# Conditioning by columns, rotary tables loaded early, the context's keys after the first gate tile, and squares added up on TensorE

## The chip, the cores and the metric

The kernel runs on one core of a Trainium2 chip. The metric is the device time of one execution in microseconds (us), as the median of several executions; lower is better. The engines are named as the profile names them: PE (TensorE's matmuls), PEld (its weight loads), DVE (VectorE), ACT (ScalarE), POOL (GpSimd), SP (the engine that issues the DMAs).

## What is computed

Two layers of a diffusion backbone over 1024 latent tokens of width 1024, with 256 context tokens. The change touches only the start of the first layer: the modulation from the two conditioning vectors `c` and `c_ctx`, the RMSNorms of latents and context, and keys and values. Cut to that, the reference is:

```
def rms_norm(x, g):
    y = x * lax.rsqrt(jnp.mean(x * x, axis=-1, keepdims=True) + EPS)
    return y * g

def adaln(cvec, w_mod, b_mod):
    return jnp.split(jax.nn.silu(cvec) @ w_mod + b_mod, 6, axis=-1)

# layer 0
sh1, sc1, gt1, sh2, sc2, gt2 = adaln(c, w_mod[0], b_mod[0])
csh1, csc1, ...              = adaln(c_ctx, w_mod[0], b_mod[0])
xm = rms_norm(h, g_mix[0]) * (1.0 + sc1) + sh1        # 1024 latent tokens
xc = rms_norm(ctx, g_mix[0]) * (1.0 + csc1) + csh1    # 256 context tokens
q, k, v, su, sv = split_in_proj(xm @ w_in)
q  = apply_axial_rope(rms_norm(q, q_gain), rope)
k  = apply_axial_rope(rms_norm(k, k_gain), rope)
kc, vc = jnp.split(xc @ w_in[:, k and v columns], 2)
kc = rms_norm(kc, k_gain)                             # no rotation
attn = block_attention(q, concat([kc, k]), concat([vc, v]))
sg   = spatial_gating(gelu(su), gelu(sv), w_sp, b_sp)
h = h + gt1 * (concat([attn, sg]) @ w_out)            # then the FFN, then layer 1
```

## The kernel before

Features lie on the 128 partitions (eight tiles, k = 0 to 7) and tokens run along the free axis; the latents come in two halves of 512 tokens, `xA` and `xB`, the context as `xhC` (eight tiles of 256). Every product of wide matrices is split in high and low parts and made of three matmuls (`mm3`, L180).

**Conditioning** (L245 to L314). The first 2048 of the modulation's columns (shift and scale) are needed first. Their weights `wma` come in eight blocks of 1 MB, one for each k. For three quarters of the columns, PE multiplies with `s2v[:, k, :]` (the two silu'd vectors, two columns) as the stationary operand and 512 columns of weights as the moving one, into three rows `mps` (L277); for the last quarter DVE forms weighted sums `macc` (L254, L256), whose columns PE adds up with a vector of ones (`col_sums`, L185). ACT copies the rows `mps` out (`mrow`, L305), PE turns them in twelve transposes (L308), and `mcol` then holds all shifts and scales as columns. DVE makes `mod`, `modc` and the gains `gp` of it (L299, L310, L311).

**Norms.** `sumsq` squares each tile on ACT (L207) and adds the squares on DVE (L211); `rstd_bcast` has PE add up the columns (`ps_v`, L185), DVE scales (`nv`, L196), POOL takes the power (`nr`, L140), and PE spreads the result over the partitions (`rb`, L200). That is done for `xA` inside the conditioning loop, later for the context and for `xB` (`normalize`, L219 to L227, which also writes the modulated high and low parts `xcm` and `xm[1]`). `xA` gets its modulation by `shift` and `parts` (L386 to L397) and becomes `xm[0]`.

**Tables.** `gains` and `rope` are loaded after that (L371, L375), and POOL multiplies them to four tables (`tab`, L380), which the keys (`rotate`, L442, L445) need.

**Keys, values, gate** (L514 to L526). `wkv` is the weight of keys and values; `kv_tile(kt)` handles 128 tokens (24 matmuls of 256 columns); kt 0 and 1 are the context, 2 to 5 the first half, 6 to 9 the second. `su_half(0, wu, 0)` is the first gate tile `u` (48 matmuls of 512 columns, `ups`). The order written is kt 2 to 5, kt 0 and 1, `u`, kt 6 to 9.

Two things set the order of the work: each engine runs its own list in order, and a scheduler of the tile framework makes these lists from the program, by its own estimates, before anything runs. Pools limit how far ahead an engine may go: squares and the later modulation weights `wmb` share three buffers (`npool`), weights `w` share four (`wpool`) with the `wma` blocks k = 4 to 7, and unconverted weights `raw` have three.

Of the kernel before, what the change touches and what calls it, by code (L numbers as in the profile page):

```python
# [18 lines left out]
P = 128  # L19
# [33 lines left out]
def hybrid_kernel(  # L53
# [35 lines left out]
    def htile(name="h", n=HALF):  # L89
        return hpool.tile([P, NB], F32, name=name, tag="h")[:, 0:n]  # L90
# [4 lines left out]
    def xtile(n=HALF, name="x"):  # L95
        return xpool.tile([P, NB], F32, name=name, tag="x")[:, 0:n]
# [86 lines left out]
    def col_sums(out, a):  # L183

        nc.tensor.matmul(out=out, lhsT=a, rhs=ones[:, 0:1], start=True, stop=True)  # L185


    def rstd_bcast(s, n, scale):

        at = [min(o, n - P) for o in range(0, n, P)]  # L190
        nj = len(at)
        ps = psc(nj, "ps_v")
        for j, o in enumerate(at):
            col_sums(ps[:, j:j + 1], s[:, o:o + P])
        v = sm(nj, "nv")
        nc.vector.tensor_scalar(out=v, in0=ps, scalar1=scale, scalar2=EPS, op0=ALU.mult, op1=ALU.add)  # L196
        r = rsqrt_small(v, nj, "nr")
        rb = psc(n, "rb")
        for j, o in enumerate(at):
            nc.tensor.matmul(out=rb[:, o:o + P], lhsT=r[:, j:j + 1].broadcast_to([P, P]), rhs=ident, start=True, stop=True)  # L200
        return rb

    def sumsq(tiles, n, alloc=ntile):
        s = None
        for t in tiles:
            q = alloc(n, "sq")
# [9 lines left out]
    def new_xm(half):  # L216
        xm[half] = [blk("xm") for _ in range(KD)]

    def normalize(tiles, n, g, b, outs, inplace):  # L219

        rb = rstd_bcast(sumsq(tiles, n), n, 1.0 / D)
        for k, t in enumerate(tiles):
            y = t if inplace else ntile(n, "xh")
            (hi, lo), gk, bk = outs(k), g[:, k:k + 1], b[:, k:k + 1]
            nc.vector.scalar_tensor_tensor(out=y, in0=t, scalar=gk, in1=rb, op0=ALU.mult, op1=ALU.mult)
            nc.scalar.activation(hi, y, AF.Identity, bias=bk)  # L226
            nc.vector.scalar_tensor_tensor(out=lo, in0=y, scalar=bk, in1=hi.bitcast(F32), op0=ALU.add, op1=ALU.subtract)  # L227

    def normalize_xm(half, tiles, g, b, cs=slice(0, HALF), inplace=False):
        normalize(tiles, cs.stop - cs.start, gp[:, g:g + KD], mod[:, b:b + KD],  # L230
                  lambda k: (xm[half][k][:, 0, cs], xm[half][k][:, 1, cs]), inplace)

    def load_pairs(half, k0, n):
        out = []
        for k in range(k0, k0 + n):
            if k % 2 == 0:
                t = blk("xp", F32)
            nc.sync.dma_start(out=t[:, k % 2, :], in_=xT[half, k])
            out.append(t[:, k % 2, :])
        return out  # L240
# [5 lines left out]
    s2 = const.tile([P, 16], F32, name="s2")  # L246
    nc.scalar.activation(s2, col(C_C2, 16), AF.Silu)
    s2v = s2.rearrange("p (k two) -> p k two", two=2)
    mps = [psa(name="mps") for _ in range(3)]
    macc = [xtile(name="macc") for _ in range(2)]  # L250

    def weighted_add(acc, w, cs, first):
        if first:
# [2 lines left out]
            nc.vector.scalar_tensor_tensor(out=acc, in0=w, scalar=cs, in1=acc, op0=ALU.mult, op1=ALU.add)  # L256

    xA = []
    for k in range(KD):
        if k < 4:  # L260
            ws = []
            for i in range(2):
                t = blk("wma", F32)
                nc.sync.dma_start(out=t, in_=wm_a[k][:, i * 1024:(i + 1) * 1024].rearrange("p (a b) -> p a b", a=2))
                ws += [t[:, 0, :], t[:, 1, :]]
        else:
            t = wpool.tile([P, 2048], F32, name="wma", tag="w")
            nc.sync.dma_start(out=t, in_=wm_a[k])
            ws = [t[:, j * 512:(j + 1) * 512] for j in range(4)]
        if k in (1, 3):  # L270
            xA += load_pairs(0, 2 * (k - 1), 4)
        if k == 5:
            wqueue.append(w_in[2])
            wqueue.extend(w_in[{"q": 0, "u": 3, "v": 5}[kind] + g] for kind, g in STAGES)
            wqueue.extend(w_out[g] for _ in range(2) for g in range(4))
        for j in range(3):
            nc.tensor.matmul(out=mps[j][0:2, :], lhsT=s2v[:, k, :], rhs=ws[j], start=(k == 0), stop=(k == KD - 1))  # L277
        for e in range(2):
            weighted_add(macc[e], ws[3], s2v[:, k, e:e + 1], k == 0)
        if k == 4:  # L280
            rbA = rstd_bcast(sumsq(xA, HALF), HALF, 1.0 / D)
    mcol = psc(32, "mcol")
    for i in range(4):
        for e in range(2):
            col_sums(mcol[:, 24 + 2 * i + e:25 + 2 * i + e], macc[e][:, i * P:(i + 1) * P])
    wready.append(prep(wqueue.popleft()))
    for t in xA:
        nc.vector.tensor_tensor(out=t, in0=t, in1=rbA, op=ALU.mult)
# [10 lines left out]
        nc.vector.scalar_tensor_tensor(out=gp[:, dst:dst + 8], in0=sc, scalar=1.0, in1=col(g, 8),  # L299
                                       op0=ALU.add, op1=ALU.mult)  # L300

    mrow = []
    for j in range(3):
        t = htile("mrow")
        nc.scalar.activation(t[0:2, :], mps[j][0:2, :], AF.Copy)  # L305
        mrow.append(t)
    for i in range(12):
        nc.tensor.transpose(mcol[:, 2 * i:2 * i + 2], mrow[i // 4][0:2, (i % 4) * P:(i % 4 + 1) * P], ident[0:2, 0:2])  # L308
    mcv = mcol.rearrange("p (i two) -> p i two", two=2)
    nc.vector.tensor_tensor(out=mod[:, 0:16], in0=mcv[:, :, 0], in1=col(C_BMOD, 16), op=ALU.add)  # L310
    nc.vector.tensor_tensor(out=modc, in0=mcv[:, :, 1], in1=col(C_BMOD, 16), op=ALU.add)  # L311
# [58 lines left out]
    gt = htile("gt")  # L370
    nc.sync.dma_start(out=gt[:, 0:256], in_=gains.partition_broadcast(P))  # L371
    rt = []
    for i in range(2):
        t = htile("rt")
        nc.sync.dma_start(out=t, in_=rope[i])  # L375
        rt.append(t)

    def table(i, g):
        t = htile("tab")
        nc.gpsimd.tensor_tensor(out=t.rearrange("p (t d) -> p t d", d=HD),  # L380
                                in0=rt[i].rearrange("p (t d) -> p t d", d=HD),
                                in1=gt[:, g * HD:(g + 1) * HD].unsqueeze(1).broadcast_to([P, 8, HD]), op=ALU.mult)
        return t
# [15 lines left out]
    for k in range(0, KD, 2):  # L399
# [1 line left out]
        shift(k + 1)  # L401
        parts(k + 1)
        parts(k)
    kC, kS, qC, qS = table(0, 2), table(1, 3), table(0, 0), table(1, 1)
    xcm = [blk("xcm") for _ in range(4)]

    def xc_dst(k):
# [1 line left out]
        sl = slice((k % 2) * CTX, (k % 2 + 1) * CTX)  # L409
        return b[:, 0, sl], b[:, 1, sl]  # L410

    normalize(xhC, CTX, gp[:, 8:16], modc[:, 0:8], xc_dst, True)
    new_xm(1)
    normalize_xm(1, xB, 0, SH1, inplace=True)

    def lat(k, tt):
        b = xm[tt // 4][k]
# [783 lines left out]
```

## Time and profile before

| | us |
|---|---|
| median of three runs | 2373.87 (2371.97 to 2375.66) |
| the profiled execution | 2372.76 |
| its span on the core | 2371.0 |

| engine | busy us | share of the span |
|---|---|---|
| PE | 2327.0 | 98% |
| PEld | 1978.2 | 83% |
| DVE | 1628.5 | 69% |
| ACT | 918.5 | 39% |
| POOL | 411.1 | 17% |

The profile gives, for each stretch, how long an engine was busy and which clock TensorE was granted: 1.00 is 2.4 GHz, 0.50 is 1.2 GHz. A float32 matmul stands in it as two records. A timeline row is a run of like instructions: start, length, engine, line, what is written and read, shapes, count, and in brackets how long the engine had idled before and what ended that. The two RMSNorms, the modulation and the keys lie in the first 90 of 2371 us.

### The profile page before, as it was taken

What the parts mean: (1) busy time and instruction counts of PE and PEld (TensorE: products, weight loads), DVE (VectorE), ACT (ScalarE), POOL (GpSimd) and SP (SyncE); (2) the same over time, 40 slices, a digit from 0 to 9 for tenths busy, and PEclk for the clock granted to TensorE, in tenths of its full rate; (3) what the DMA queues carried; (4) which work ended last, traced back from release to release, by engine and by line L of the source; (5) the groups of instructions that cost most, each with busy time, mean ns of one, the idle gap of its engine ahead of it and who ended that gap; (6) DMA issues with size and microseconds to landing.
All of it is one profiled execution on the core that took longest, in us unless ns stands there. A gap on an engine that the chain in (4) does not pass through costs nothing.

```text
span 2371.0 us, 31670 instructions
## 1 busy us (share of the span) xinstructions
PE 2327.0 (98%) x12396; PEld 1978.2 (83%) x12396; DVE 1628.5 (69%) x2515; ACT 918.5 (39%) x1480; POOL 411.1 (17%) x405
## 2 busy tenths in 40 slices
PE   7999899999999999999999999999999999999998
PEld 3899677777888888888888788888878989999998
DVE  6887777656545666447999966999986555444357
ACT  4542688843211222234333455333445433222222
POOL 2362677820000000001112300002230000000000
PEclk9899999999999999999999999999999999999999
DMA  8451000042222455332222242222233222222222
GB/s 307 136 194 55 19 1 1 6 148 96 101 77 89 160 194 174 121 126 88 94 93 89 91 166 98 89 98 90 97 98 121 96 96 89 90 90 89 90 90 98
DMA packets 79573, 245.68 MB, mean 104 GB/s; under 512 B 8512, under 2 KB 12864, under 8 KB 78912
## 3 DMA queue, kind: packets, MB, share of 16 engines
q1 hardware_dynamic: 79424, 243.66, 30.4%
q8 instruction: 97, 1.59, 0.3%
q14 instruction: 52, 0.43, 0.1%
HBM read 235.24 MB, written 8.39 MB: 103 GB/s over the span
## 4 chain that ended last, share of the span: by engine, by line
PE 73%; DVE 12%; issue 2%; POOL 1%; ACT 1%; DMA 0%; DVEq 0%; ACTq 0%; POOLq 0%
PE gu L180 35%; PE fo L180 17%; PE pw L180 8%; DVE conv L999 7%; PE wo L180 4%; DVE w L113 2%; PE mx L628 2%; PE st L650 1%; PE st L649 1%; PE o L676 1%; PE o L674 1%; PE o L675 1%; POOL pacc L993 1%; DVE h L791 0%; DVE conv L1002 0%
## 5 line engine op out<-in xcount | busy, mean ns | idle before, releaser
L180 PE MATMUL gu<-xm,w 128*128 128x512 f32 (+2 forms) x5280 | 997.8, 350 | 1.9 <-ACT xm L226 1.9
L180 PEld LDWEIGHTS gu<-xm,w 128*128 128x128 f32 x5280 | 854.4, 188 | 135.0 <-ACT xm L226 2.1
L112 ACT ACTIVATE w<-raw 128x1024 fp32r<-128x1024 f32 x324 | 340.6, 1056 | 556.7 <-issue 237.7
L113 DVE TENSOR_TENSOR w<-raw,w 128x1024 fp32r<-128x1024 f32 x324 | 406.8, 1259 | 192.4 <-ACT w L112 191.8
L180 PE MATMUL fo<-act,w 128*128 128x512 f32 (+2 forms) x2640 | 499.8, 350 | 1.5 <-DVE act L113 1.5
L180 PEld LDWEIGHTS fo<-act,w 128*128 128x128 f32 x2640 | 428.3, 189 | 65.7 <-DVE act L113 1.9
L999 DVE SCALAR_TENSOR_TENSOR conv<-glu,pc,conv 128x496 f32<-128x496 f32 (+1 forms) x400 | 316.6, 836 | 0.3
L791 DVE SCALAR_TENSOR_TENSOR h<-fo,mod,h 128x264 f32<-128x264 f32 (+2 forms) x256 | 159.6, 631 | 96.7 <-PE fo L180 95.9
L993 POOL TENSOR_TENSOR pacc<-pacc,ptmp 128x496 f32<-128x496 f32 (+1 forms) x64 | 109.0, 1703 | 450.7 <-ACT pacc L989 398.3
L180 PE MATMUL pw<-xm,w 128*128 128x512 f32 x768 | 178.7, 394 | 0.0
L180 PEld LDWEIGHTS pw<-xm,w 128*128 128x128 f32 x768 | 144.1, 188 | 33.5
L841 DVE TENSOR_TENSOR silu<-gu,silu 128x512 f32<-128x512 f32 (+2 forms) x110 | 63.8, 580 | 141.0 <-PE gu L180 140.8
L840 ACT ACTIVATE silu<-gu 128x512 f32<-128x512 f32 (+2 forms) x110 | 56.2, 511 | 260.4 <-PE gu L180 260.4
L140 POOL TENSOR_TENSOR nr<-nv,mhalf 128x4 f32<-128x4 f32 (+2 forms) x16 | 16.4, 1027 | 803.3 <-DVE nv L196 803.3
L630 DVE TENSOR_REDUCE mp<-mx 128x1 f32<-128x512 f32 (+1 forms) x192 | 112.1, 598 | 24.6 <-PE mx L628 21.6
L112 ACT ACTIVATE act<-silu 128x512 fp32r<-128x512 f32 (+2 forms) x110 | 59.1, 537 | 143.6 <-DVE silu L841 143.6
L665 POOL TENSOR_TENSOR pb<-p,pb 128x512 fp32r<-128x512 f32 x80 | 104.3, 1304 | 5.3
L256 DVE SCALAR_TENSOR_TENSOR acc<-raw,s,acc 128x512 f32<-128x512 f32 x84 | 62.9, 749 | 45.2 <-DMA raw<-in_wm_b_dram 44.1
L180 PE MATMUL pw<-sw,w 128*128 128x264 f32 (+1 forms) x576 | 91.4, 320 | 0.0
L180 PE MATMUL wo<-cat,w 128*128 128x512 f32 x384 | 89.9, 394 | 0.7 <-DVE cat L113 0.7
L969 POOL MEMSET glu<- 128x15 f32 x16 | 0.9, 112 | 510.6 <-PE fo L180 510.6
L180 PEld LDWEIGHTS pw<-sw,w 128*128 128x128 f32 x576 | 83.0, 188 | 7.2
(169 smaller groups left out, 2450.3 us busy)
## 6 DMA issues: line engine op xcount, KB each, us to landing
raw<-in_ffn_in_dram SPq DMA_DIRECT2D x164, 512.0 KB, 3.6
raw<-in_ffn_out_dram SPq DMA_DIRECT2D x82, 512.0 KB, 3.6
raw<-in_wm_b_dram SPq DMA_DIRECT2D x48, 512.0 KB, 3.7
raw<-in_pw_dram SPq DMA_DIRECT2D x48, 512.0 KB, 3.7
wmb<-in_wm_b_dram SPq DMA_DIRECT2D x64, 256.0 KB, 2.8
raw<-in_w_out_dram SPq DMA_DIRECT2D x16, 512.0 KB, 3.6
raw<-in_w_in_dram SPq DMA_DIRECT2D x14, 512.0 KB, 4.6
wma<-in_wm_a_dram SPq DMA_DIRECT2D x8, 512.0 KB, 7.9
```

The source lines that it names most:

```text
L112: nc.scalar.activation(dst_hi, src, AF.Copy)
L113: nc.vector.tensor_tensor(out=dst_lo, in0=src, in1=dst_hi.bitcast(F32), op=ALU.subtract)
L180: nc.tensor.matmul(out=ps, lhsT=a, rhs=b, start=(i == 0), stop=(i == n - 1))
L256: nc.vector.scalar_tensor_tensor(out=acc, in0=w, scalar=cs, in1=acc, op0=ALU.mult, op1=ALU.add)
L628: pin(nc.tensor.matmul(out=ps, lhsT=b[:, 0, j * P:(j + 1) * P], rhs=kst1[:, kv, o:o + n], start=True, stop=True))
L630: chained(nc.vector.tensor_reduce(out=mp[:, 3 * j + s:3 * j + s + 1], in_=ps, axis=AX.X, op=ALU.max))
L665: chained(eng.tensor_tensor(out=t[:, 1, :], in0=p, in1=t[:, 0, :].bitcast(F32), op=ALU.subtract))
L791: nc.vector.scalar_tensor_tensor(out=h, in0=ps, scalar=gc, in1=h, op0=ALU.mult, op1=ALU.add)
L840: nc.scalar.activation(sg, ps, AF.Silu)
L841: nc.vector.tensor_tensor(out=sg, in0=ps, in1=sg, op=ALU.mult)
L993: nc.gpsimd.tensor_tensor(out=pacc, in0=pacc, in1=tmp, op=ALU.add)
L999: nc.vector.scalar_tensor_tensor(out=out, in0=g[:, t:t + n], scalar=wc(t), in1=out, op0=ALU.mult, op1=ALU.add)
```

## The change

Four edits, none of which alters what is computed.

1. The rows `mps`, the sums `macc`, the copies `mrow` and the transposes go. For every k PE multiplies 16 times with a 128x128 block of the weights as the stationary operand and the two columns `s2v[:, k, :]` as the moving one, straight into `mcol`, which is accumulated over k: 128 matmuls of two columns.
2. The loads of `gains` and `rope` and the four table products move up into the loop, to k = 1.
3. `su_half(0, wu, 0)` is written ahead of the context's `kv_tile(0)` and `kv_tile(1)`.
4. The norms of the context and of `xB` no longer add squares on DVE: `square_sums` has PE multiply each tile of squares, as 128x128 stationary blocks, with one column of ones, accumulating over the eight tiles: 16 such column sums for the context and 32 for `xB`, in place of 2 and 4.

```diff
+    def square_sums(tiles, n):
+        at = [min(o, n - P) for o in range(0, n, P)]
+        ps = psc(len(at), "ps_v")
+        for i, t in enumerate(tiles):
+            q = ntile(n, "sq")
+            nc.scalar.activation(q, t, AF.Square)
+            for j, o in enumerate(at):
+                nc.tensor.matmul(out=ps[:, j:j + 1], lhsT=q[:, o:o + P], rhs=ones[:, 0:1], start=(i == 0 and j == 0),
+                                 stop=(i == len(tiles) - 1), skip_group_check=True)
+        return ps, at
...
-        rb = rstd_bcast(sumsq(tiles, n), n, 1.0 / D)
+        rb = rstd_bcast((sums or sumsq)(tiles, n), n, 1.0 / D)
...
-    mps = [psa(name="mps") for _ in range(3)]
-    macc = [xtile(name="macc") for _ in range(2)]
+    mcol = psc(32, "mcol")
...
+        if k == 1:
+            gt = htile("gt")
+            nc.sync.dma_start(out=gt[:, 0:256], in_=gains.partition_broadcast(P))
+            rt = []
+            for i in range(2):
+                t = htile("rt")
+                nc.sync.dma_start(out=t, in_=rope[i])
+                rt.append(t)
+            kC, kS, qC, qS = table(0, 2), table(1, 3), table(0, 0), table(1, 1)
...
-        for j in range(3):
-            nc.tensor.matmul(out=mps[j][0:2, :], lhsT=s2v[:, k, :], rhs=ws[j], start=(k == 0), stop=(k == KD - 1))
-        for e in range(2):
-            weighted_add(macc[e], ws[3], s2v[:, k, e:e + 1], k == 0)
+        for i in range(16):
+            nc.tensor.matmul(out=mcol[:, 2 * i:2 * i + 2], lhsT=ws[i // 4][:, (i % 4) * P:(i % 4 + 1) * P],
+                             rhs=s2v[:, k, :], start=(k == 0 and i == 0), stop=(k == KD - 1),
+                             skip_group_check=True)
...
-    mcol = psc(32, "mcol")
-    for i in range(4):
-        for e in range(2):
-            col_sums(mcol[:, 24 + 2 * i + e:25 + 2 * i + e], macc[e][:, i * P:(i + 1) * P])
...
-    mrow = []
-    for j in range(3):
-        t = htile("mrow")
-        nc.scalar.activation(t[0:2, :], mps[j][0:2, :], AF.Copy)
-        mrow.append(t)
-    for i in range(12):
-        nc.tensor.transpose(mcol[:, 2 * i:2 * i + 2], mrow[i // 4][0:2, (i % 4) * P:(i % 4 + 1) * P], ident[0:2, 0:2])
...
-    normalize(xhC, CTX, gp[:, 8:16], modc[:, 0:8], xc_dst, True)
+    normalize(xhC, CTX, gp[:, 8:16], modc[:, 0:8], xc_dst, True, square_sums)
     new_xm(1)
-    normalize_xm(1, xB, 0, SH1, inplace=True)
+    normalize_xm(1, xB, 0, SH1, inplace=True, sums=square_sums)
...
+    wu = next_w()
+    su_half(0, wu, 0)
     for kt in range(0, 2):
         kv_tile(kt)
     flush()
-    wu = next_w()
-    su_half(0, wu, 0)
```

The scheduler orders the first 110 us anew. The first place is PE during the conditioning. It stood so (a row is a run of like instructions with its count; `mps` and `mcol` are the conditioning, `ps_v` column sums of squares, `rb` a norm's spreading, `kvps` keys and values):

```order
L277 MATMUL mps<-wma,s_101 2x512 x12
L185 MATMUL ps_v<-ones,sq 128x1 x4
L277 MATMUL mps<-wma,s_101 2x512 x3
L200 MATMUL rb<-ident,nr 128x128 x4
L277 MATMUL mps<-wma,s_101 2x512 x9
L185 MATMUL mcol<-ones,macc 128x1 x8
L308 MATMUL mcol<-ident,mrow 128x2 x12
L180 MATMUL kvps<-w,xm 128x256 x30
```

and stands so now:

```order
L314 MATMUL mcol<-s_101,wma 128x2 x80
L185 MATMUL ps_v<-ones,sq 128x1 x4
L314 MATMUL mcol<-s_101,wma 128x2 x14
L218 MATMUL rb<-ident,nr 128x128 x4
L314 MATMUL mcol<-s_101,wma 128x2 x34
L196 MATMUL ps_v<-ones,sq 128x1 x10
```

The `rb` of `xA` has moved behind 14 of the 16 matmuls of k = 5, and ten of the context's column sums stand between the conditioning and the first `kvps`. The second place is PE from there to the `rb` of `xB`. Before, behind the 30 `kvps` (first the context's sums and `rb`, then its keys and values, `kvps<-w,xcm`, with the sums and the `rb` of `xB` among them):

```order
L185 MATMUL ps_v<-ones,sq 128x1 x2
L180 MATMUL kvps<-w,xm 128x256 x38
L200 MATMUL rb<-ident,nr 128x128 x2
L180 MATMUL kvps<-w,xm 128x256 x28
L180 MATMUL kvps<-w,xcm 128x256 x24
L185 MATMUL ps_v<-ones,sq 128x1 x4
L180 MATMUL kvps<-w,xcm 128x256 x19
L200 MATMUL rb<-ident,nr 128x128 x4
```

and now, behind 22 `kvps` and `ups` matmuls, the context's other six sums and two `kvps`:

```order
L180 MATMUL kvps<-w,xm 128x256 x23
L218 MATMUL rb<-ident,nr 128x128 x2
L196 MATMUL ps_v<-ones,sq 128x1 x12
L180 MATMUL kvps<-w,xm 128x256 x11
L196 MATMUL ps_v<-ones,sq 128x1 x4
L180 MATMUL kvps<-w,xm 128x256 x6
L196 MATMUL ps_v<-ones,sq 128x1 x12
L180 MATMUL kvps<-w,xm 128x256 x7
L196 MATMUL ps_v<-ones,sq 128x1 x4
L180 MATMUL kvps<-w,xm 128x256 x25
L218 MATMUL rb<-ident,nr 128x128 x4
```

The 32 sums of `xB` lie in four lots among the `kvps` of kt 2 to 5; the context's `kvps` have left this piece and follow the 48 `ups` behind it. The third place is ACT from the squares of `xA` on. Before:

```order
L207 ACTIVATE sq<-xp 128x512 x8
L112 ACTIVATE w<-raw 128x1024 x2
L305 ACTIVATE mrow<-mps 2x512
L207 ACTIVATE sq<-xc 128x256 x3
L305 ACTIVATE mrow<-mps 2x512 x2
L207 ACTIVATE sq<-xc 128x256 x3
L392 ACTIVATE xp<-xp,mod,gp 128x512
```

and now (`w` is a weight's high part, `xp<-xp,mod,gp` the first `shift` of `xA`):

```order
L225 ACTIVATE sq<-xp 128x512 x8
L194 ACTIVATE sq<-xc 128x256 x2
L112 ACTIVATE w<-raw 128x1024
L194 ACTIVATE sq<-xc 128x256
L112 ACTIVATE w<-raw 128x1024 x3
L402 ACTIVATE xp<-xp,mod,gp 128x512
L194 ACTIVATE sq<-xc 128x256
L406 ACTIVATE xm<-xp 128x512
```

All four weight conversions now stand ahead of the first `shift`; each writes into a buffer that a `wma` block (k = 4, 5, 6, 7) holds until PE has read it. On DVE the first low part `w` now stands ahead of the `nv` that the `rb` of `xA` hangs on. Behind the first 110 us PE's order is the same as before.

## Rows read from the trace of the kernel before

**Rows 1.** Windows by stage: stretch, length, busy of PE, PEld, DVE, ACT, POOL, clock, DMA.
```profile
0.00:41.00 41.00, 30.58 (x92) 8.62 (x92) 23.71 (x40) 11.95 (x20) 5.47 (x10) 0.96 0.97 371
41.00:78.00 37.00, 29.56 (x171) 28.27 (x172) 32.31 (x73) 21.23 (x50) 15.30 (x12) 0.72 0.38 133
78.00:228.00 150.00, 149.91 (x1073) 140.12 (x1071) 127.72 (x316) 58.94 (x164) 65.80 (x87) 1.00 0.41 135
228.00:258.00 30.00, 23.09 (x147) 20.07 (x146) 23.26 (x55) 13.50 (x23) 17.09 (x17) 0.89 0.17 54
258.00:2371.00 2113.00, 2093.89 (x10921) 1781.15 (x10919) 1421.53 (x2036) 812.91 (x1224) 307.45 (x280) 1.00 0.29 96
```

**Rows 2.** Timeline of PE from 5 to 50 us, the conditioning.
```profile
5.94 8.20 PE L277 MATMUL mps<-wma,s 128*2 128x512 f32 x12 [5.94 <-DMA wma<-in_wm_a_dram]
...
23.87 1.05 PE L185 MATMUL ps_v<-ones,sq 128*128 128x1 f32 x8 [3.09 <-DVE sq L211]
...
30.30 7.89 PE L277 MATMUL mps<-wma,s 128*2 128x512 f32 x18
38.12 1.95 PE L185 MATMUL mcol<-ones,macc 128*128 128x1 f32 x16
...
44.16 6.13 PE L180 MATMUL kvps<-w,xm 128*128 128x256 f32 x30 [3.26 <-ACT xm L396]
```

**Rows 3.** Timeline of PE from 63 to 136 us.
```profile
63.75 5.12 PE L180 MATMUL kvps<-w,xcm 128*128 128x256 f32 x22 [2.57 <-DVE xcm L227]
68.86 1.84 PE L185 MATMUL ps_v<-ones,sq 128*128 128x1 f32 x8
71.37 4.42 PE L180 MATMUL kvps<-w,xcm 128*128 128x256 f32 x19 [0.67 <-ACT qn L433]
75.60 1.55 PE L200 MATMUL rb<-ident,nr 128*128 128x128 f32 x8
...
82.12 6.96 PE L180 MATMUL ups<-xm,w 128*128 128x512 f32 x29
...
117.01 19.09 PE L180 MATMUL qps<-w,xm 128*128 128x256 f32 x159
```

**Rows 4.** Windows, PE alone: stretch, length, busy, granted clock, DMA.
```profile
45.00:49.00 4.00, 4.00 (x20) 0.50 0.23 93
...
64.00:68.00 4.00, 4.00 (x19) 0.50 0.04 6
69.00:71.00 2.00, 1.70 (x8) 0.50 0.40 134
72.00:76.00 4.00, 4.00 (x20) 0.50 0.46 159
78.00:82.00 4.00, 4.00 (x19) 1.00 0.55 180
```

**Rows 5.** Timeline of PEld, two of the first weight loads.
```profile
11.02 0.13 PEld L277 LDWEIGHTS mps<-wma,s 128*2 128x2 f32 x1 [0.73 <-issue]
...
12.26 0.09 PEld L277 LDWEIGHTS mps<-wma,s 128*2 128x2 f32 x1 [0.34 <-issue]
```

**Rows 6.** Timeline of ACT from 34 to 44 us.
```profile
34.24 1.06 ACT L112 ACTIVATE w<-raw 128x1024 fp32r<-128x1024 f32 x1 [0.19 <-DMA raw<-in_w_in_dram]
...
37.00 1.01 ACT L207 ACTIVATE sq<-xc 128x256 f32<-128x256 f32 x3
...
41.88 0.80 ACT L392 ACTIVATE xp<-xp,mod,gp 128x512 f32<-128x512 f32 x1
...
42.96 1.15 ACT L396 ACTIVATE xm<-xp 128x512 fp32r<-128x512 f32 x2
```

**Rows 7.** Timeline of DVE: weights' low parts, and the scaling of `xB`.
```profile
36.77 2.35 DVE L113 TENSOR_TENSOR w<-raw,w 128x1024 fp32r<-128x1024 f32 x2
...
79.33 5.35 DVE L225 SCALAR_TENSOR_TENSOR xp<-xp,gp,rb 128x512 f32<-128x512 f32 x8
```

**Rows 8.** Timeline of POOL: the first power, and the tables.
```profile
25.97 1.03 POOL L140 TENSOR_TENSOR nr<-nv,mhalf 128x4 f32<-128x4 f32 x1 [20.76 <-DVE nv L196]
44.97 10.11 POOL L380 TENSOR_TENSOR tab<-rt,gt 128x512 f32<-128x512 f32 x4 [17.96 <-DMA rt<-in_rope_dram]
```

More of the change, by code (lines that the diff above doesn't have):

```diff
@@ L185, in col_sums @@
         nc.tensor.matmul(out=out, lhsT=a, rhs=ones[:, 0:1], start=True, stop=True)
+    def square_sums(tiles, n):
[8 more added lines that the diff above has]
+        return ps, at
     def rstd_bcast(s, n, scale):
+        if isinstance(s, tuple):
+            return rstd_of(*s, n, scale)
         at = [min(o, n - P) for o in range(0, n, P)]
@@ L194, in rstd_bcast, with rstd_of @@
             col_sums(ps[:, j:j + 1], s[:, o:o + P])
+        return rstd_of(ps, at, n, scale)
+    def rstd_of(ps, at, n, scale):
+        nj = len(at)
         v = sm(nj, "nv")
@@ L217, in new_xm, with normalize @@
         xm[half] = [blk("xm") for _ in range(KD)]
-    def normalize(tiles, n, g, b, outs, inplace):
-        rb = rstd_bcast(sumsq(tiles, n), n, 1.0 / D)
+    def normalize(tiles, n, g, b, outs, inplace, sums=None):
+        rb = rstd_bcast((sums or sumsq)(tiles, n), n, 1.0 / D)
         for k, t in enumerate(tiles):
@@ L227, in normalize, with normalize_xm @@
             nc.vector.scalar_tensor_tensor(out=lo, in0=y, scalar=bk, in1=hi.bitcast(F32), op0=ALU.add, op1=ALU.subtract)
-    def normalize_xm(half, tiles, g, b, cs=slice(0, HALF), inplace=False):
+    def normalize_xm(half, tiles, g, b, cs=slice(0, HALF), inplace=False, sums=None):
         normalize(tiles, cs.stop - cs.start, gp[:, g:g + KD], mod[:, b:b + KD],
-                  lambda k: (xm[half][k][:, 0, cs], xm[half][k][:, 1, cs]), inplace)
+                  lambda k: (xm[half][k][:, 0, cs], xm[half][k][:, 1, cs]), inplace, sums)
     def load_pairs(half, k0, n):
@@ L258, in hybrid_kernel, with table @@
     xA = []
+    def table(i, g):
+        t = htile("tab")
+        nc.gpsimd.tensor_tensor(out=t.rearrange("p (t d) -> p t d", d=HD),
+                                in0=rt[i].rearrange("p (t d) -> p t d", d=HD),
+                                in1=gt[:, g * HD:(g + 1) * HD].unsqueeze(1).broadcast_to([P, 8, HD]), op=ALU.mult)
+        return t
     for k in range(KD):
@@ L368, in hybrid_kernel @@
     v2 = kvpool.tile([P, NKT * 2, HD], F32R, name="v2")
[L370 to L383, printed above, removed]
     new_xm(0)
@@ L403, in hybrid_kernel @@
         parts(k)
-    kC, kS, qC, qS = table(0, 2), table(1, 3), table(0, 0), table(1, 1)
     xcm = [blk("xcm") for _ in range(4)]
```

## The prediction

> **What bounds the kernel now.** I read the windows by stage first [rows 1]. From 258 us to the end PE is busy 2093.9 of 2113 us at the full clock, and from 78 to 228 us 149.9 of 150: work that leaves DVE or ACT there is worth nothing, and what the change can win or lose has to come from the first 78 us. There PE is idle or slow: 30.6 of the first 41 us busy, then 29.6 of 37 at a mean clock of 0.72. Next, PE's own timeline of that part [rows 2, 3]. Conditioning starts at 5.94, when the first weights land, and ends 3.26 us before 44.16, so at 40.90; the first key matmul starts at 44.16. From there the 96 matmuls of kt 2 to 5, the 48 of the context and the 48 of the first gate tile `u` last until 82.12 + 6.96 = 89.1. Last, the clock [rows 4]: 0.50 from 45 to 49 and again from 64 to 76, though PE was busy in nearly all of that. So three times are to be worked out: the end of the conditioning (40.9), the first key matmul (44.2), and the end of these 192 matmuls (89.1). Behind that PE is dense, and whatever the third time moves, the end moves.
>
> **Prices.** A column sum (two records: each loads 128x128 weights, then moves one column) costs 1.95/8 = 0.244 us at the full clock [rows 2] and 1.84/4 = 0.46 at 0.50 [rows 3, 4]. The new `mcol` matmuls have the same weights and move two columns instead of one; both ends of their price are these, 0.244 and 0.46. A matmul of 256 columns costs 19.09/159 = 0.120, one of 512 columns 6.96/29 = 0.240 [rows 3]. The old form cost 7.89/9 = 0.88 for each of three matmuls per k, 2.6 us [rows 2]; the new one costs 16 x 0.244 = 3.9 or 16 x 0.46 = 7.4. So PE's share of the conditioning grows in either case, and what leaves DVE (`macc`) was not what PE waited for at the end.
>
> **Which clock?** The first weight loads follow each other at half the later pace (0.73 us of issue time before the one at 11.02, 0.34 before the one at 12.26 [rows 5]), so PE starts at 1.2 GHz and comes to 2.4 only after some 5 us of moving 512 columns at a time. In the new program there is no such stretch before the first key matmul. What do column sums do to the clock? The best row is the stretch from 63.75 [rows 3, 4]: key matmuls, then eight records of column sums from 68.86 to 70.7, an idle of 0.67 us, key matmuls again; the clock stays at 0.50 all through, until after 76, 12 us after the start, while from 71.37, where only matmuls with many columns follow, it takes about 5 us. I take it that a stretch of nothing but these narrow matmuls leaves the clock at 1.2 GHz. The Trainium skill ("TensorE: Matmul & The Clock Gate", What's actually happening) says that the clock is set by how busy PE has recently been, without telling weight loads from columns; by that, a dense stretch of narrow matmuls would raise it, and the sum would be the first rival's 2385 instead of 2409. No row here shows such a stretch as long as the new one.
>
> **The change, part by part.**
>
> *A, the end of the conditioning.* 128 x 0.46 = 58.9 us, and inside it four column sums (1.84) and one `rb` (1.55 [rows 3]): 5.94 + 62.3 = 68.2. No wait adds to that: at 371 GB/s [rows 1] all conditioning weights, with `xA` and the 0.64 MB of tables now ahead of them (11.4 MB), have landed by about 31 us, and PE comes to the last block at 60.8. 68.2 against 40.9: +27.3. The copies, transposes and `macc` sums that go (some 2.8 us behind the last `mps`) are in these two ends.
>
> *B, to the first key matmul.* PE has ten column sums of the context in front of it, 4.6 us at half clock. Beside it ACT must convert the last weight (its buffer is held until the last `mcol` matmul), 1.06, then `shift` 0.80, two squares 0.34 each, two high parts 0.57 each [rows 6]: 3.7. So 4.6 against 3.26: +1.3, first key matmul at 72.8.
>
> *C, the 192 matmuls.* Before: 89.1 - 44.2 = 44.9. Now, at full clock: 144 x 0.120 = 17.3, 48 x 0.240 = 11.5, the remaining 38 column sums x 0.244 = 9.3, six `rb` matmuls 2.3: 40.4. On top: the clock needs about 5 us to rise from 72.8, which loses 2.5. Then the piece with the 32 sums of `xB`: 7.8 us of sums with 2.9 of key matmuls strewn in, and 25 key matmuls (3.0) behind. If the clock doesn't fall it loses nothing; if the whole piece runs at half, 13.7; I take 7.5, about the middle, because the clock needs some us to fall and the last 25 matmuls to raise it. Behind the `rb` of `xB`, DVE scales `xB` (5.35 [rows 7]) and makes its low parts, with adaLN additions between; PE has 17.3 us of `u` and context work as cover for that. A wait of 0 to 4 us; I take 2. Sum: 40.4 + 2.5 + 7.5 + 2 = 52.4 against 44.9, +7.5. What the change wins is in here: the waits for the context's tiles (2.57 and 0.67 [rows 3]) and half of the slow stretch from 64 to 76 are gone, since `u` covers them. The 42 additional column sums (10.2 us at full clock) take that back.
>
> *D, tables.* POOL was idle from the start until 25.97 [rows 8], so the 10.1 us of tables fit in there; they no longer hold up the context's `nr`, which PE hardly waited for. The moved loads delay `xA`, weights and context by 0.64 MB / 371 GB/s = 1.7 us, hidden under A. Nothing.
>
> *E, later.* From 110 us on PE's order is the same. The waits from 228 to 258 (30 - 23.1 = 6.9 us [rows 1]) hang on work in that place and move along.
>
> **Sum:** 27.3 + 1.3 + 7.5 = +36, on the profiled execution's 2372.8: 2409. That execution lies 1.1 us under the median of the runs, so the choice of base doesn't matter. Bounds of this case: with no fall of the clock and no wait in C, 27.3 + 1.3 - 2.0 = +27 (2399); with the whole piece at half and 4 us of waits, 27.3 + 1.3 + 15.7 = +44 (2417).
>
> **Rivals.**
>
> *The clock rises under narrow matmuls.* For: nothing between them idles. Against: the stretch from 64 to 76. Then k = 0 to 4 keep up with the loads and end about 30 (the fifth block lands near 26, plus 3.9), column sums 31, 14 matmuls 34.3. There PE waits: `rb` hangs on POOL's `nr` (1.03 [rows 8]), that on `nv`, which stands on DVE behind a weight's low part (1.18 [rows 7]), that on ACT's conversion (1.06), which stands behind two squares of the context (0.68); before, the context's first square came at 37.0 [rows 6]. 37.0 + 0.7 + 1.1 + 1.2 + 0.2 + 1.0 = 41.2, `rb` until 42.7, 34 matmuls 8.3, and 2.4 for a clock that fell in the 7 us of waiting: 53.4. ACT's chain 3.7: first key matmul at 57.1. C at 40.4, plus 2 for the wait above and 2 because `nv` of `xB` stands behind `wmb` additions: 101.5 against 89.1, +12.4: 2385, between 2380 and 2392 (34 matmuls at half clock to the end). So this case is slower too.
>
> *Faster: a narrow matmul costs next to nothing.* If PE loaded the next weights under the current ones, the price p would lie far below 0.244. With `rb` at 42.7 as above, the third time is 42.7 + 34p + 3.7 + 31.1 + 38p + 4 = 81.5 + 72p. It equals 89.1 at p = 0.105, and at p = 0.03 it is 83.7: 5.4 us faster, 2367. Against: the column sums at 23.87 and 38.12 [rows 2] are this form, back to back, at more than twice the deciding price.
>
> *Even.* The first rival, and a PE that arrives 12 us later finds its weights and vectors ready between 228 and 258: of 6.9 us of waits there most go. 12.4 - 6.9 = 5.5, and without C's two waits 1.5: about 2375. For it speaks only that the waits there hang on loads and conversions; against it, that these start when buffers come free, which moves along.
>
> **How the numbers follow.** Clock low: 0.70, at 2409. First rival: 0.20, at 2385. Even: 0.07. Faster: 0.03. A measurement here can tell about 0.2% (4.7 us) from no change. Slower by more than that: 0.90; within: 0.07; faster: 0.03. The range has to reach to the first rival, since the likeliest case alone holds too little: 2380 to 2416 leaves out the other two rivals and the tails of the first two cases, together about 2 in 10. The likeliest case's own range is 2399 to 2417.
>
> **What would show it.** In the profile after: PE's `mcol` stretch, 128 matmuls as 256 records, at 0.23 each and granted clock 0.50 or at the pace of a cold start, with its end near 68 (0.122 and near 53 in the first rival, with an idle before `rb` that ends on `nr`); first key matmul near 73 (57); the end of the first `u` tile and the context's keys near 125 (101); lots of column sums from 80 to 105 at clock 0.50; from there to the end the same distance as before, 2371.0 - 89.1 = 2281.9. The prediction is wrong if `mcol` ends before 45, if the third time lies under 94, or if the distance from there to the end changes by more than 5 us.

## The result and the profile after

The changed kernel takes 2402.4 us (median of four runs, 2398.7 to 2404.7) against 2373.0 for the kernel before: 1.0121 times as long, with a 95% interval of 1.0103 to 1.0138. That is 29.4 us more; 36 were forecast, and the likeliest case's own range, 2399 to 2417, held it. The profiled execution took 2402.5 us, with a span of 2400.7.

PE's own timeline of the kernel after, its first 118 us (columns as in [rows 2]):

```profile
6.16 34.26 PE L314 MATMUL mcol<-s,wma 128*128 128x2 f32 x160 [6.16 <-DMA wma<-in_wm_a_dram]
40.28 1.84 PE L185 MATMUL ps_v<-ones,sq 128*128 128x1 f32 x8
41.98 6.11 PE L314 MATMUL mcol<-s,wma 128*128 128x2 f32 x28
47.96 2.05 PE L218 MATMUL rb<-ident,nr 128*128 128x128 f32 x8
49.80 14.51 PE L314 MATMUL mcol<-s,wma 128*128 128x2 f32 x68
64.17 4.41 PE L196 MATMUL ps_v<-ones,sq 128*128 128x1 f32 x20
68.44 2.05 PE L180 MATMUL kvps<-w,xm 128*128 128x256 f32 x8
...
77.82 2.74 PE L196 MATMUL ps_v<-ones,sq 128*128 128x1 f32 x24
...
83.88 5.11 PE L196 MATMUL ps_v<-ones,sq 128*128 128x1 f32 x24
...
116.52 0.30 PE L491 MATMUL ktp<-ident,kr 128*128 128x128 f32 x1 [2.30 <-DVE v L113]
...
117.94 2.33 PE L180 MATMUL kvps<-w,xm 128*128 128x256 f32 x10
```

The last of these points in the kernel before:

```profile
88.92 2.30 PE L180 MATMUL kvps<-w,xm 128*128 128x256 f32 x18
```

From 6.16 to 64.2 PE hardly idles, and moves two columns at a time: 0.214 us per record, 0.428 per matmul. Where before the conditioning ended at 40.9, it now ends 23.3 later. Ten column sums follow, 4.4 us, and the first key matmul stands at 68.44 instead of 44.16 [rows 2]. The second half's keys, which came at 88.92, begin at 117.94, and all 29.0 us of the difference are there. From that point to the end it is 2282.8 us, against 2282.1 before: behind it 0.7 us were lost.

Five windows of PE in the kernel after (columns: window, its length, PE busy and records, granted clock, DMA share, GB/s):

```profile
6.00:40.00 34.00, 33.84 (x159) 1.00 1.02 392
50.00:64.00 14.00, 14.00 (x69) 1.00 0.23 75
74.00:77.00 3.00, 3.00 (x27) 1.00 0.02 5
83.00:96.00 13.00, 13.00 (x63) 0.50 0.34 118
98.00:109.00 11.00, 11.00 (x51) 1.00 0.37 129
```

The two groups of 24 sums in the timeline, one before and one in the window from 83 to 96, say what that window's clock costs: the same work takes 2.74 us at 77.82 and 5.11 at 83.88, 0.114 and 0.213 per record. PE is busy through all 13 us between 83 and 96, and the clock is at 1.2 GHz nevertheless. The conditioning's 0.214 per record is that second pace, though the view prints 1.00 for it: no clock below 1.00 stands in it before the fall at 82.8, so it shows the cold start as full speed, as it does for the kernel before at 6 to 12 us. The pace is not that of the loads: it is the same while they fill the DMA engines (share 1.02, 6 to 40 us) and behind them (0.23, 50 to 64).

### The profile page after: what moved, and what is told of

Same layout as the page of the kernel before. It is cut to its first block, busy times and chain, and to the rows that moved or that the text cites. A ratio compares the mean times of both kernels' runs of the same rounds, so it can differ in the third digit from the quotient of the medians.

```text
span 2400.7 us, 32145 instructions
## 1 busy us (share of the span) xinstructions
PE 2366.0 (99%) x12660; PEld 2040.8 (85%) x12660; DVE 1608.7 (67%) x2485; ACT 917.1 (38%) x1477; POOL 414.0 (17%) x405
## 4 chain that ended last, share of the span: by engine, by line
PE 80%; DVE 6%; issue 1%; POOL 1%; ACT 1%; DMA 0%; DVEq 0%; ACTq 0%; POOLq 0%
PE gu L180 37%; PE fo L180 18%; PE pw L180 11%; PE wo L180 4%; DVE conv L1008 3%; PE st L659 1%; PE st L658 1%; PE mx L637 1%; PE o L685 1%; PE o L683 1%; PE o L684 1%; DVE w L113 1%; PE ps_v L185 0%; PE rb L218 0%; PE vps L180 0%
## 5 line engine op out<-in xcount | busy, mean ns | idle before, releaser
L1002 POOL TENSOR_TENSOR pacc<-pacc,ptmp 128x496 f32<-128x496 f32 (+1 forms) x64 | 116.7, 1823 | 443.0 <-ACT pacc L998 392.7
L850 DVE TENSOR_TENSOR silu<-gu,silu 128x512 f32<-128x512 f32 (+2 forms) x110 | 64.2, 584 | 141.0 <-PE gu L180 141.0
L273 DVE SCALAR_TENSOR_TENSOR acc<-raw,s,acc 128x512 f32<-128x512 f32 x84 | 63.0, 750 | 44.3 <-DMA raw<-in_wm_b_dram 43.2
L180 PE MATMUL wo<-cat,w 128*128 128x512 f32 x384 | 89.8, 394 | 0.7 <-DVE cat L113 0.7
```

The lines of the kernel that those rows point to most:

```text
L180: nc.tensor.matmul(out=ps, lhsT=a, rhs=b, start=(i == 0), stop=(i == n - 1))
L850: nc.vector.tensor_tensor(out=sg, in0=ps, in1=sg, op=ALU.mult)
L1002: nc.gpsimd.tensor_tensor(out=pacc, in0=pacc, in1=tmp, op=ALU.add)
```

## The experiments

Four kernels undo or do parts; then one size is changed, the number of columns that a narrow matmul moves. The times of the three points that the prediction works with, from PE's timelines (conditioning ends, first key matmul, first key matmul of the second half), in us:

| kernel | conditioning | first key | second half | median of all runs |
|---|---|---|---|---|
| before | 40.9 | 44.2 | 88.9 | 2373.0 |
| after | 64.2 | 68.4 | 117.9 | 2402.4 |
| e1, old conditioning | 43.7 | 47.5 | 98.1 | 2378.9 |
| e2, columns only | 64.2 | 68.6 | 113.2 | 2398.7 |
| e3, moves only | 43.2 | 46.4 | 83.2 | 2374.0 |
| e4, no square sums | 64.2 | 67.4 | 101.3 | 2387.3 |
| e5, 32 columns | 63.6 | 67.9 | 121.9 | 2406.1 (one run) |
| e6, 128 columns | 42.5 | 45.9 | 93.9 | 2379.0 (one run) |
| e8, `u` split | 40.6 | 43.8 | 84.4 | 2377.0 |
| e9, all wide | 41.5 | 45.0 | 82.8 | 2368.4 |
| e10, wide, no square sums | 42.5 | 46.9 | 80.3 | 2373.5 |
| e13, 128 columns only | 42.9 | 47.8 | 89.8 | 2374.2 |

The kernel before stood at 2372.5 to 2374.0 beside them.

### One part at a time

**e1** is the changed kernel with the old rows, `macc`, copies and transposes, so with the edits 2 to 4:

```diff
-    mcol = psc(32, "mcol")
+    mps = [psa(name="mps") for _ in range(3)]
+    macc = [xtile(name="macc") for _ in range(2)]
...
-        for i in range(16):
-            nc.tensor.matmul(out=mcol[:, 2 * i:2 * i + 2], lhsT=ws[i // 4][:, (i % 4) * P:(i % 4 + 1) * P],
...
+        for j in range(3):
+            nc.tensor.matmul(out=mps[j][0:2, :], lhsT=s2v[:, k, :], rhs=ws[j], start=(k == 0), stop=(k == KD - 1))
...
```

> The changed kernel with the old conditioning (rows and weighted sums); early tables, u ahead of the context and column sums of squares stay. Theory (most of the loss is the conditioning, whose narrow matmuls run at 1.2 GHz): conditioning ends near 42, the 192 matmuls of keys and first u tile near 95 instead of 117.9, some 2379 us, at most 8 over the kernel before. Rival (the 42 additional column sums and the clock that falls among them are the loss, the conditioning is hidden by loads): near 2400, as the changed kernel.

Measured: 2378.9, ratio 1.0029 (1.0017 to 1.0040). The columns cost 23.5 of the 29.4 us. Most of the rest is edit 4: e3 below differs from e1 in that edit alone and is 4.9 us faster. The sums are 20 records ahead of the first key matmul (3.95 us) and 76 among the keys, where the granted clock is 0.50 from 61.5 to 74.9.

**e2** is the reverse, the kernel before with edit 1 alone:

```diff
-        for j in range(3):
-            nc.tensor.matmul(out=mps[j][0:2, :], lhsT=s2v[:, k, :], rhs=ws[j], start=(k == 0), stop=(k == KD - 1))
...
+        for i in range(16):
+            nc.tensor.matmul(out=mcol[:, 2 * i:2 * i + 2], lhsT=ws[i // 4][:, (i % 4) * P:(i % 4 + 1) * P],
...
```

> The kernel before with the conditioning by columns alone. Theory: conditioning ends near 64 instead of 40.9, keys start near 68, and since more is ready by then the end moves by less than the 23 us, by 18 to 23: 2391 to 2396. Rival (sums are the loss): within 5 us of the kernel before.

Measured: 2398.7, ratio 1.0111 (1.0096 to 1.0126), 3 us above the expected span. Its conditioning ends where the changed kernel's does. What I had not counted is a wait of 6.9 us in front of the second context tile:

```profile
96.39 5.38 PE L180 MATMUL kvps<-w,xcm 128*128 128x256 f32 x24 [6.93 <-ACT qn L423]
```

The context's keys stand ahead of `u` there, and PE has to wait until ACT has normalised an earlier tile's keys (`qn`). In the changed kernel edit 3 has `u` in that place, so the parts do not simply add up.

**e3** has edits 2 and 3 without 1 and 4: the loads and tables early, and `u` ahead of the context's keys.

```diff
...
+    wu = next_w()
+    su_half(0, wu, 0)
     for kt in range(0, 2):
         kv_tile(kt)
     flush()
-    wu = next_w()
-    su_half(0, wu, 0)
```

> The kernel before with early tables and with u ahead of the context's keys, and nothing else of the change. Theory: the waits for the context's tiles and part of the stretch at 1.2 GHz from 63 to 76 us go, 5 to 9 us faster: 2364 to 2368. Rival (the reordering by the scheduler is itself harmful, and is why the changed kernel is slow): slower than the kernel before.

Measured: 2374.0, ratio 1.0007 (0.9998 to 1.0017): no gain, against my 5 to 9 us. The waits of [rows 3] are gone and PE is through with the 192 matmuls some 8 us earlier (80.7), but then it waits for the second half:

```profile
83.22 0.98 PE L180 MATMUL kvps<-w,xm 128*128 128x256 f32 x6 [2.55 <-ACT xm L244]
87.37 0.45 PE L501 MATMUL ktp<-ident,kr 128*128 128x128 f32 x1 [3.17 <-DVE hv L447]
89.11 8.20 PE L180 MATMUL kvps<-w,xm 128*128 128x256 f32 x44 [1.30 <-ACT qn L452]
```

The first query matmul comes at 114.8, in the kernel before at 112.97. The prediction had the first wait as 0 to 4 us and not the other two. `hv`, which one of them names, and `kr`, which that transpose reads, stand on DVE behind the eight scalings of `xB` (81.68 to 87.0). DVE and ACT are the bound there.

**e4** is the changed kernel without edit 4: `square_sums` is not handed over, DVE adds the squares as before.

```diff
-    normalize(xhC, CTX, gp[:, 8:16], modc[:, 0:8], xc_dst, True, square_sums)
+    normalize(xhC, CTX, gp[:, 8:16], modc[:, 0:8], xc_dst, True)
...
-    normalize_xm(1, xB, 0, SH1, inplace=True, sums=square_sums)
+    normalize_xm(1, xB, 0, SH1, inplace=True)
```

> The changed kernel with squares added up on DVE again; the rest stays. Theory: conditioning still ends near 64; without 42 column sums (10 us at full clock, 17 at half) and without the fall of the clock among them the 192 matmuls end near 102 instead of 117.9: 2385 to 2390. Rival (sums are free because PE waits for modulated tiles anyway): near 2400.

Measured: 2387.3, ratio 1.0065 (1.0048 to 1.0082), as expected, with the second half's keys at 101.3:

```profile
101.34 0.75 PE L180 MATMUL kvps<-w,xm 128*128 128x256 f32 x5
```

The clock does not fall between the first key matmul and 265 us. So edit 4 cost 15 us here, more than the 10 us that its 42 additional sums take at the full clock: with it PE ran at 0.50 from 83 to 96 us, the key matmuls between the sums too.

### One size: how many columns a matmul moves

That the clock made the difference was so far only read from the pace. **e5** and **e6** keep the 128 conditioning matmuls, their weights and the order among them, and let each move its two columns 16 or 64 times over. e6:

```diff
-    mcol = psc(32, "mcol")
+    mcw = [psa(name="mcol") for _ in range(4)]
+    mcb = [mcw[i // 4][:, P * (i % 4):P * (i % 4 + 1)] for i in range(16)]
+    s2w = s2v.unsqueeze(2).broadcast_to([P, KD, 64, 2])
...
-            nc.tensor.matmul(out=mcol[:, 2 * i:2 * i + 2], lhsT=ws[i // 4][:, (i % 4) * P:(i % 4 + 1) * P],
-                             rhs=s2v[:, k, :], start=(k == 0 and i == 0), stop=(k == KD - 1),
+            nc.tensor.matmul(out=mcb[i], lhsT=ws[i // 4][:, (i % 4) * P:(i % 4 + 1) * P],
+                             rhs=s2w[:, k], start=(k == 0 and i % 4 == 0), stop=(k == KD - 1),
...
```

> The changed kernel; each of the 128 conditioning matmuls moves 32 columns (its two, 16 times over) instead of 2, with the same weights; the result is the same. By the rows of the old form (512 columns: 0.44 us per record at the full clock) 32 columns are about 0.03 us of a record. Theory one, the clock stays low there because hardly a column moves: 32 columns are between the cases; more likely still low, about 0.21 us per record and an end of the conditioning near 64, total 2402. Rival, the pace of 0.21 belongs to the form (a weight load for every matmul) and not to the clock: the same 0.21 here, and again 0.21 or more with 128 columns.

> As the last one, with 128 columns moved by each conditioning matmul (its two, 64 times over; about 0.11 us of a record by the rows of the old form). Theory one, the clock is low because hardly a column moves: here, with 64 times as many columns, it rises within the conditioning, the records go from about 0.22 to 0.12-0.14 us each, the conditioning ends between 50 and 56 instead of 64, and the total is 2388 to 2395: more work in less time. Rival, the pace belongs to the form: 0.21 or more to the end, conditioning end 64 or later, total 2402 or more.

PE's timeline of e5, one row, and of e6, up to the end of the conditioning:

```profile
5.58 34.31 PE L316 MATMUL mcol<-s,wma 128*128 128x32 f32 x160 [5.58 <-DMA wma<-in_wm_a_dram]
```

```profile
5.97 10.13 PE L316 MATMUL mcol<-s,wma 128*128 128x128 f32 x64 [5.97 <-DMA wma<-in_wm_a_dram]
17.25 7.41 PE L316 MATMUL mcol<-s,wma 128*128 128x128 f32 x64 [1.15 <-DMA wma<-in_wm_a_dram]
26.12 1.05 PE L185 MATMUL ps_v<-ones,sq 128*128 128x1 f32 x8 [1.46 <-DVE sq L229]
27.17 3.84 PE L316 MATMUL mcol<-s,wma 128*128 128x128 f32 x32
30.84 1.05 PE L218 MATMUL rb<-ident,nr 128*128 128x128 f32 x8
31.74 10.88 PE L316 MATMUL mcol<-s,wma 128*128 128x128 f32 x96
```

With 32 columns nothing changes: 0.214 per record, 2406.1 us. With 128, 64 times as many as the change moves, the first 64 records still start at the slow pace, the next 64 take 0.116 each, and PE now waits for the weights to land. The conditioning ends at 42.5 instead of 64.2: more work in 22 us less. The rival of a fixed price of the form is out. The total fell by 23 us, more than I expected, because I had put the end at 50 to 56. Not all of that need be the clock: the scheduler also orders e6 anew. `rb` stands behind 80 of the matmuls there and not behind 94, and on DVE `nv` (27.21) is no longer behind a weight's low part (37.02). What the clock did without another order, e7 and e12 show.

In e6 the square sums are as narrow as in the changed kernel, and the clock is at 0.50 again from 59.7 to 76.5:

```profile
60.00:76.00 16.00, 16.00 (x77) 0.50 0.25 84
```

**e7** and **e12** put the question where nothing else on PE changes: 64 sums nobody needs, in the dense stretch of query matmuls of the kernel before, with one column each (e7, the diff) and with 128 (e12, where `rhs=ones`).

```diff
     def q_tile(g, tt, wq):
+        if g == 0 and tt == 5:
+            dum = psc(64, "dum")
+            for i in range(64):
+                tc.keep_in_program_order(nc.tensor.matmul(out=dum[:, i:i + 1], lhsT=ident, rhs=ones[:, 0:1],
+                                                          start=(i == 0), stop=(i == 63), skip_group_check=True))
```

> The kernel before, with 64 additional column sums (128 records, 128x128 weights, one column, into an accumulator that nothing reads) one behind the other in the dense stretch of query matmuls near 125 us, where the clock has been full for 40 us. Theory one: the first 5 us or so at 0.122 per record, then the granted clock falls to 0.50 and the rest goes at 0.21, though PE never idles; the stretch takes 22 to 25 us, some query matmuls behind it run at half too, and the total is 2396 to 2400. Rival, a dense engine keeps its clock whatever it moves: 0.122 to the end, 15.6 us, clock 1.00, total 2388.

> The kernel before with the same 64 additional sums in the same dense stretch as in the run with narrow sums there, each moving 128 columns instead of 1. Theory (the few columns, not the weight loads, let the clock fall): the clock stays at 1.00, the 128 records take 15 to 16 us instead of 25.1, total 2387 to 2391. Rival (a stretch with a weight load for every matmul lowers the clock): it falls again, 25 us, total about 2400.

e7, PE's timeline around the sums, and windows in and behind them (columns as above):

```profile
115.37 10.59 PE L180 MATMUL qps<-w,xm 128*128 128x256 f32 x87
125.80 25.14 PE L533 MATMUL dum<-ones,ident 128*128 128x1 f32 x128
150.80 10.86 PE L180 MATMUL qps<-w,xm 128*128 128x256 f32 x72
```

```profile
126.00:128.00 2.00, 2.00 (x20) 1.00 0.45 149
130.00:150.00 20.00, 20.00 (x96) 0.50 0.16 54
150.00:155.00 5.00, 5.00 (x25) 0.50 0.00 0
156.00:161.00 5.00, 5.00 (x44) 1.00 0.00 0
```

e12, the same two views:

```profile
125.66 14.45 PE L533 MATMUL dum<-ones,ident 128*128 128x128 f32 x128
139.87 8.75 PE L180 MATMUL qps<-w,xm 128*128 128x256 f32 x72
```

```profile
128.00:140.00 12.00, 12.00 (x110) 1.00 0.35 118
```

In e7 PE had run at the full clock since 73.6 us and does not idle for a moment, and 2.4 us into the narrow sums the clock falls to 0.50. It comes back at 155.5, among the query matmuls, which pay 10.86 - 8.75 = 2.1 us. With 128 columns the same number of weight loads and matmuls takes 14.45 us instead of 25.14 and the clock stays. Totals 2400.3 and 2385.0, one run each. So being busy in the records did not keep TensorE's clock here: behind matmuls that moved one column it fell, behind the same ones with 128 columns it did not. The Trainium skill ("TensorE: Matmul & The Clock Gate", What's actually happening) ties the clock to how busy PE has recently been; the window from 130 to 150, 20.00 of 20 us busy at 0.50, does not bear that out if busy is what the profile counts as busy.

### A version that beats both

**e9** is e6 with the sums of the three norms in front (and of the later ones) widened too: `ones` in place of `ones[:, 0:1]`, and 128 columns of PSUM for each sum.

```diff
-        nc.tensor.matmul(out=out, lhsT=a, rhs=ones[:, 0:1], start=True, stop=True)
+        nc.tensor.matmul(out=out, lhsT=a, rhs=ones, start=True, stop=True)
...
-                nc.tensor.matmul(out=ps[:, j:j + 1], lhsT=q[:, o:o + P], rhs=ones[:, 0:1], start=(i == 0 and j == 0),
+                nc.tensor.matmul(out=ps[:, j * P:(j + 1) * P], lhsT=q[:, o:o + P], rhs=ones, start=(i == 0 and j == 0),
...
```

> The changed kernel with 128 columns moved by each conditioning matmul, and now also by each column sum of the three norms in front (the sums of squares); same results. Theory (narrow matmuls hold the clock low, wide ones with the same weights do not): the half-clock stretches from 46 to 49 and from 60 to 76 us go, the sums cost 0.12 to 0.14 us per record, the first gate tile and the context's keys end at 84 to 87 instead of 93.9, total 2369 to 2374. Rival, the sums between key matmuls lower the clock whatever they move: the stretch from 60 to 76 stays, total 2377 to 2381.

Measured: 2368.4 (2366.9 to 2371.1), ratio 0.9976 (0.9967 to 0.9985) to the kernel before: 5.5 us faster than that, 34 faster than the change as it stood, with the same number of matmuls. PE's timeline of e9, some rows, and a window:

```profile
41.45 1.95 PE L196 MATMUL ps_v<-ones,sq 128*128 128x128 f32 x16
43.64 1.16 PE L196 MATMUL ps_v<-ones,sq 128*128 128x128 f32 x8 [0.24 <-ACT sq L194]
44.98 3.09 PE L180 MATMUL kvps<-w,xm 128*128 128x256 f32 x24 [0.19 <-ACT xm L411]
...
82.76 0.99 PE L180 MATMUL kvps<-w,xm 128*128 128x256 f32 x6
84.02 0.74 PE L180 MATMUL kvps<-w,xm 128*128 128x256 f32 x4 [0.27 <-ACT xm L244]
85.34 2.32 PE L180 MATMUL kvps<-w,xm 128*128 128x256 f32 x14 [0.59 <-DVE xm L245]
```

```profile
45.00:65.00 20.00, 20.00 (x171) 1.00 0.31 103
```

The clock stays at 1.00 from there until 244 us. The 192 matmuls take 82.76 - 44.98 = 37.8 us; before they took 44.8.

**e10** is e9 with DVE adding the squares, to see whether edit 4 is then worth its place (the diff of e4 on top of e9).

> As the last one, without the change's sums of squares on TensorE: DVE adds the squares up as in the kernel before, so PE has 42 column sums less. Theory one: PE's part of the 192 matmuls is 34 us instead of 40, u and the context end near 80, and the second half's tiles come 3 to 6 us too late for it, as in the run with the moves alone; total 2367 to 2373, at or a little below the kernel before. Rival: what TensorE's sums save DVE is worth more than their 6 us on PE, because DVE is the bound between 50 and 95 us; total above that of the run before this one by 2 us or more.

Measured: 2373.5, ratio 1.0001 (0.9992 to 1.0010), 5 us above e9, so the rival held. PE reaches the second half 2.5 us earlier than in e9 and waits more:

```profile
46.48 0.71 PE L185 MATMUL ps_v<-ones,sq 128*128 128x128 f32 x4 [3.98 <-DVE sq L229]
...
83.22 6.26 PE L180 MATMUL kvps<-w,xm 128*128 128x256 f32 x47 [2.33 <-DVE xm L245]
...
93.28 3.09 PE L180 MATMUL kvps<-w,xm 128*128 128x256 f32 x24 [1.08 <-ACT qn L447]
...
98.17 5.83 PE L180 MATMUL ups<-xm,w 128*128 128x512 f32 x24 [1.70 <-ACT qn L447]
```

With wide sums, edit 4 wins 5 us; with narrow ones it cost 15 (and 4.9 beside the old conditioning, e1 against e3).

**e13** is the kernel before with edit 1 alone, 128 columns wide (the diff of e6 on top of e2).

> The kernel before with the conditioning as columns alone, 128 columns moved by each of its matmuls. With 2 columns the same edit cost 26 us. Theory: nearly all of that was the clock; with 128 columns the conditioning ends 1 to 2 us behind the kernel before (42 to 43), the first key matmul starts near 46 and the total is 2371 to 2377. Then the 5.5 us which the all-wide kernel wins come from the change's other parts. Rival: DVE, without the weighted sums, is early enough to win the 5 us by itself: total 2366 to 2370.

Measured: 2374.2, ratio 1.0003 (0.9993 to 1.0013). The 26 us that e2 lost are gone, and nothing is won: the 4 us wait of e10 for DVE's context squares stands here too:

```profile
46.95 1.01 PE L185 MATMUL ps_v<-ones,sq 128*128 128x1 f32 x4 [3.98 <-DVE sq L211]
```

So the 5.5 us of e9 come with edit 4, on top of the others, which by themselves win nothing (e10, e13). Whether edit 4 needs edits 2 and 3 for that, no run shows.

**e8** asked whether a smaller move would do in the kernel before: half of `u` ahead of the context's keys, half behind.

```diff
...
+    wu = next_w()
+    su_half(0, wu, 0, (0,))
     for kt in range(0, 2):
         kv_tile(kt)
     flush()
-    wu = next_w()
-    su_half(0, wu, 0)
+    su_half(0, wu, 0, (1,))
```

> The kernel before with one part of the change halved: the first gate tile u is split, 24 of its matmuls ahead of the context's keys and 24 behind them, nothing else. Theory: putting all 48 ahead (tried as part of the moves alone) only moved PE's wait from the context's tiles to the second half's; with 24 on either side both have 5.8 us of cover. The waits of 2.6 and 0.7 us before the context's key matmuls go, the clock does not fall there, kt 2 to 5, u and context end at 80 to 83 instead of 88.9, total 2364 to 2367, ratio 0.997. Rival, what is won in front is given back behind, as with the moves alone: the total stays within 2371 to 2375.

Measured: 2377.0, ratio 1.0014 (1.0005 to 1.0024); my theory fell, and the rival's upper end was passed by 2 us.

```profile
68.90 4.53 PE L180 MATMUL kvps<-w,xcm 128*128 128x256 f32 x24 [3.24 <-ACT u L504]
...
86.46 4.04 PE L180 MATMUL kvps<-w,xm 128*128 128x256 f32 x32 [1.56 <-ACT qn L433]
```

PE reaches the second half's keys 4.5 us earlier than before, after a new wait of 3.2 us on ACT ahead of the context; and from there to 104 us it waits at six places, 6.9 us in all, for ACT and DVE.

## Why the prediction was right, step by step

- **What bounds, and which three times.** Held. The whole difference stands at the third time, 117.94 against 88.92, and the distance to the end changed by 0.7 us.
- **The clock under narrow matmuls** was the choice that decided. It was taken from eight records between key matmuls [rows 3, 4], and there the clock could have been kept down by the idle time around them. e7 shows the clock fall without any idle time; with 128 columns it rises in e6 and stays up in e12. The first rival, a clock that rises under narrow matmuls, is refuted.
- **A, 68.2 forecast, 64.2 measured.** The order and the absence of waits were right; the price was a little high. 0.46 per matmul came from eight records whose modelled end is counted in (1.84/8 = 0.230); in a row of 160 records it is 0.214, and 256 x 0.016 = 4.1 us. The mean over the short row was too long by what the last one's end adds.
- **B, +1.3 forecast, +1.0 measured** (68.44 - 64.2 against 3.26). Behind the ten sums PE does not wait: ACT's first two high parts are done at 67.8.
- **C, 52.4 forecast, 49.5 measured,** against 44.8 before. The clock's share was close: some 4 us at half pace after 68.44 lose 2 (2.5 forecast), and 13.6 us, from 82.8 to 96.4, lose 6.8 (7.5). The wait came at 2.3 us (2), but that is luck: it was not for `xm[1]`, but for a transpose `ktp` whose `kr` stands on DVE behind additions that wait for their `wmb` weights to land (0.95 us before 112.56, 1.24 before 114.56). What was too high is the work at full clock. 49.5 - 2 - 6.8 - 2.3 leaves 38.4 instead of 40.4 (e9 takes 37.8 for it, with two sums less): six `rb` matmuls cost about 1.3 us, and I had priced them at 2.3 by a row that the profile shows at half clock; the rest is again the ends of short rows.
- **D, nothing** for the tables, held: POOL was through with them at 20.5 us, and `nr` did not wait for them.
- **E, nothing later,** held: 0.7 us.
- **The sum,** 36 forecast, 29.4 measured: A was 4.0 too high, B 0.3 and C 2.9, and E 0.7 too low. Most of that is the price taken from short rows and from `rb` at half clock; the mechanism held.
- **The two cases that are not slower** were put at 0.10 together. What I did not see is that the change's loss lay in the width of its moving operands, and that edit 4, freed of the slow clock, wins 5 us.
- **The first rival's own price** stays untested. It put the conditioning's end at 53.4 with a clock that rises, on a chain over ACT and DVE to `nr`; with the clock up, `rb` comes at 30.84 in e6 and the end at 42.5, but in e6's order that chain does not stand in front of `nr`.

## What to carry to other kernels

A long row of matmuls with a full block of weights and hardly a column to move ran at the half clock here (0.214 us per record with 2 columns and with 32), and the matmuls behind it paid as well (2.1 us in e7). Price such a row at that pace until a trace of your own shows another, and try moving more columns (copies of the same ones) before giving the idea up, since with 128 of them a record took no longer here than one with a single column at the full clock. Judge a part of a change only once the clock around it is the same: edit 4 costs 15 us or wins 5. And a wait taken away in front, while DVE and ACT are the bound in the same stretch, comes back a few us further on (e3, e8).

## What the runs showed of the hardware

- A float32 record with 128x128 weights takes 0.114 to 0.116 us at the full clock whether it moves 1 column (24 records in 2.74 us, after) or 128 (64 records in 7.41, e6).
- The granted clock fell to 0.50 in a stretch in which PE was busy without a gap (e7, 130 to 150 us), and again stood at 1.00 with 128 columns in the same place (e12).
- The four table products took 10.1 us in the kernel before, from 44.97 on [rows 8], and 5.3 in the changed one, from 15.21 on:

```profile
15.21 5.32 POOL L280 TENSOR_TENSOR tab<-rt,gt 128x512 f32<-128x512 f32 x4 [10.00 <-DMA rt<-in_rope_dram]
```

  DVE's busy time beside them (window, its length, DVE busy and instructions, then as above), in the kernel before and in the changed one:

```profile
45.00:55.00 10.00, 9.42 (x12) 0.78 0.26 91
```

```profile
15.00:20.50 5.50, 0.69 (x1) 1.00 1.00 339
```

  DVE was busy for 9.4 of 10 us there and for 0.7 of 5.5 here. That this is the reason for the difference is not shown; no run varied it alone.
